# Moving the weight units and the four large operand buffers of a transformer-style trunk into one pool at the head of SBUF

## The chip, the core and the metric

The kernel runs on one core of a Trainium2 chip. The number that counts is the device time of one execution in microseconds (us). The kernel before takes 2718.81 us, the median of three runs that lie between 2717.66 and 2721.08 us. A core has a tensor engine (PE, with weight loads shown apart as PEld), a vector engine (DVE), a scalar engine (ACT), a small general engine (POOL) and a queue engine (SP) that issues the transfers between the main memory and the on-chip memory SBUF. SBUF has 128 partitions; a tile lies at the same byte address in each of them, and addresses below are bytes within a partition.

## The reference

One layer over 2048 tokens of width 1024, all in float32. Three mixers run side by side on the same normalised input, their outputs are joined by one projection, and a squared-ReLU MLP and a gated embedding follow:

```python
xn = rmsnorm(h, norm_mix_g[i])
proj = xn @ w_in[i]                                     # 1024 -> 3200 columns, split among the mixers
att = chunked_attention(qa, ka, va, qn_g[i], kn_g[i], rel_bias[i])   # 6 heads, own chunk + 8 before
conv = conformer_conv(uc, ...)                          # GLU, 31 taps, layernorm, swish, pointwise
ret = retention(qr, kr, vr, gr, ret_gn_g[i])            # 6 heads, chunkwise recurrent
h = h + jnp.concatenate([att, conv, ret], axis=-1) @ w_o[i]
hn = rmsnorm(h, norm_ffn_g[i])
h = h + jnp.square(jax.nn.relu(hn @ w1[i])) @ w2[i]     # 1024 -> 4096 -> 1024
gate = jax.nn.sigmoid(rmsnorm(h, norm_ple_g[i]) @ w_pg[i])
h = h + gate * (p[i] @ w_ple[i])
```

## The kernel before

**Blocks and segments.** The tokens are worked in four blocks of 512 (`T`). Each block is a list of segments that follow each other on the tensor engine: `conv_proj`, the two halves of `gate` of the block before, three pairs of `att_proj` and `ret_proj`, `wo_a`, `wo_b`, then the MLP as eight groups, `ffn1(g+1)` ahead of `ffn2(g)`. The small matmuls and transposes of attention, convolution and retention (`att_mix`, `conv_mix`, `ret_mix`) are put between the matmuls of these segments at places that a planner of due times chooses; the tensor engine's order is fixed by the program.

**Three matmuls for one.** A product in float32 precision is made of three float32r matmuls. Every operand is kept as a rounded high part and a remainder: `xh`, `xl` for the activations, `w[:, 0]` and `w[:, 1]` for the weights. `mm3s` issues high times high, high times low, low times high. A matmul has a stationary operand, 128 columns that are loaded by a weight load, and a moving operand, here mostly 512 columns of 4 bytes, 2048 bytes of each partition. In the names of the profile the moving operand stands first: `acc<-hid,w` has `hid` moving and `w` stationary. In the projections of attention and retention the parts change places (`acc<-w,xh`: a weight slice moves, 384 or 512 columns of it).

**Weight units.** `wunit` (line 133 on) hands out units of 8 KB a partition, two parts by two halves by 512 columns, from six buffers (`wtile`, line 122). In the first block a unit is loaded raw, split on ACT and DVE (lines 126, 127) and kept in main memory; later it is loaded in one transfer of 1 MB (`w<-k_w...`). A unit feeds eight weight blocks, 24 matmuls. A stationary block starts at the unit's address plus a multiple of 512 bytes.

**The four large buffers.** `big(name, slot)` (line 79) gives buffers of 16 KB a partition, eight rows of 2048 bytes. Slots 0 and 1 hold `xh` and `xl`: of the layer's input, of the MLP's input (`wo_b`), and in the last block of the gate's input. Slots 2 and 3 hold the mixers' output `mh` and `ml`, then in turn the hidden activations `hid` of the MLP (even groups in slot 2, odd ones in slot 3, high parts in rows 0 to 3 and low parts in rows 4 to 7), and in blocks 0 to 2 the gate's input (`late`, also named `xh`, `xl`).

**Where they lie.** Tiles of a pool lie one behind the other in the order in which their tags are first asked for, and pools in the order in which they are made. In the built program of before:

| tile | first byte | modulo 2048 |
|---|---|---|
| six weight units `w` | 23,584 to 64,544, 8192 apart | 1056 |
| slot 0 and slot 1 | 72,736 and 89,120 | 1056 |
| slot 2 and slot 3 | 195,712 and 212,096 | 1152 |
| embedding operands `ph`, `pl` | 172,640 to 178,784, 2048 apart | 608 |

Of the kernel before, what the change touches and what calls it, by code (L numbers as in the profile page):

```python
# [12 lines left out]
F32R = mybir.dt.float32r  # L13
# [4 lines left out]
P = 128  # L18
D = 1024
S = 2048  # L20
T = 512
# [11 lines left out]
HALF = 512  # L33
# [7 lines left out]
def trunk(ctx, tc, a, out):  # L41
# [4 lines left out]
    class PE:  # L46
# [10 lines left out]
        def transpose(o, x, i):  # L57
            clk[0] += 240 / 2200.0
            tc.keep_in_program_order(nc.tensor.transpose(o, x, i))  # L59

    cpool = ctx.enter_context(tc.tile_pool(name="const", bufs=1))
    sp = ctx.enter_context(tc.tile_pool(name="sp", bufs=1))
    dram = ctx.enter_context(tc.tile_pool(name="dram", bufs=1, space=bass.MemoryType.DRAM))
# [9 lines left out]
    def stile(tag, bufs, shape, name=None, dt=F32):  # L73
        return sp.tile(list(shape), dt, tag=tag, name=name or tag, bufs=bufs)
# [2 lines left out]
        return stile("raw", 2, [P, UNIT], name)  # L77

    def big(name, slot):
        return stile(f"big{slot}", 1, [P, 8, T], name, F32R)  # L80

    def anat(name):
        return stile("anat", 5, [P, 256], name)
# [36 lines left out]


    def wtile():
        return stile("w", 6, [P, 2, 2, HALF], "w", F32R)

    def wsplit(w, x, n, eng):
        A.activation(w[:, 0, :n], x, AF.Copy)  # L126
# [6 lines left out]
    def wunit(name, i, n=HALF):  # L133
        key = name + "_".join(map(str, i))
        seen[key] = seen.get(key, 0) + 1
        with tc.high_priority(offset=AHEAD):
            u = wtile()
            if key in kept:
                nc.sync.dma_start(f(u)[:, :, :, :n], kept[key])
            else:  # L140
                raw = rawt("raw")
                nc.sync.dma_start(raw[:, : 2 * n], a[name][i])
                for c in range(2):
                    wsplit(u[:, c], raw[:, c * n : c * n + n], n, V)
        if key not in kept and seen[key] == (2 if name == "w2" or key in ("wc0", "wc1") else 1):
            wstage(key, u, n)
        return [u[:, 0], u[:, 1]]
# [114 lines left out]

    def xnorm(blk):
        xh, xl = big("xh", 0), big("xl", 1)
        cur["x"] = xh, xl
        tk = slice(blk * T, blk * T + T)
# [189 lines left out]
    def mix():  # L456
        if "m" not in cur:
            cur["m"] = big("mh", 2), big("ml", 3)
        return cur["m"]
# [228 lines left out]
    def wo_b():  # L688
        mh, ml = mix()
        h = cur["h"]  # L690
        x = cur["x2"] = big("xh", 0), big("xl", 1)
        sq = cur["sq"] = rnat("sq")
        cur["r2"] = None
        w = stream("w_ob")
        for j in range(KT):
            b = wide()
            for k in range(2):
                yield from mm3s(b, w(2 * j + k), (mh[:, 6 + k], ml[:, 6 + k]), k == 0, k == 1)
                if k == 1:
                    with tc.high_priority(offset=60):  # L700
                        V.tensor_tensor(h[j], h[j], b, ALU.add)
                    rms_split(j, 1, x, sq)
                yield cost(T) / 3
        del cur["m"]
# [214 lines left out]
    first = xnorm(0)  # L919
    raw = rawt("raw")  # L920
    u = wtile()
    with tc.high_priority(offset=3 * AHEAD):
        nc.sync.dma_start(ng, a["norm_g"])
# [132 lines left out]
```

## Time and profile before

| | |
|---|---|
| median of 3 runs | 2718.81 us (2717.66 to 2721.08) |
| the profiled execution's own time | 2718.58 us |
| its span, first to last instruction | 2716.6 us |
| PE busy | 2680.4 us (99%), 13354 matmuls |
| DVE, ACT busy | 1327.8 us (49%), 764.2 us (28%) |
| transfers | 533.36 MB, mean 196 GB/s |
| mean granted clock of the tensor engine | 0.996 |

The span leaves out 2.0 us that the execution's own time has around it. A matmul of the profile has a start and a modelled end; neighbours overlap in the pipeline, so that a matmul is shown with some 390 ns although the next one starts some 230 ns later. How fast the tensor engine goes is therefore read from starts: the distance from the start of one group of matmuls to the start of the next, divided by their number. The chain of work in order of time gives its pieces just so, from start to start.

### The profile page before, as it was taken

To read this page: it belongs to the slowest core of one execution; us is meant where nothing else is said; L and a number is where in the kernel's file an instruction comes from. 1 tells how busy PE (TensorE), PEld (TensorE's weight loads), DVE (VectorE), ACT (ScalarE), POOL (GpSimd) and SP (SyncE) were. 2 spreads that over 40 slices of the span, in tenths; PEclk is the share of its full clock that TensorE was granted. 3 is DMA by queue.
4 is the path that set the end of the run, shared out by engine and by line. 5 is a ranking of instruction groups with operands and counts; after the bars stand their busy time and mean duration, and the time that the engine had idled before them with its cause. 6 is when DMAs were issued, how large, how long until landed. Compare 5 with 4: busy or idle time off the path is not lost.

```text
span 2716.6 us, 33597 instructions
## 1 busy us (share of the span) xinstructions
PE 2680.4 (99%) x13354; PEld 2216.5 (82%) x13354; DVE 1327.8 (49%) x2649; ACT 764.2 (28%) x1576; POOL 97.0 (4%) x98
## 2 busy tenths in 40 slices
PE   8989999999999999999999999999999999999999
PEld 7777788888888888888888888888888888888887
DVE  7966544458655443334755552222384545222233
ACT  4444423343244222123214331101222432110111
POOL 1010000000010000000001000000000100000000
PEclk9999999999999999999999999999999999999999
DMA  8667656467633567677543455555654354555553
GB/s 285 211 213 244 219 177 208 166 198 267 217 121 140 206 216 261 216 255 261 217 168 121 159 203 192 193 186 191 240 194 170 112 199 142 189 191 187 192 201 125
DMA packets 123708, 533.36 MB, mean 196 GB/s; under 512 B 12832, under 2 KB 39712, under 8 KB 77728
## 3 DMA queue, kind: packets, MB, share of 16 engines
q1 hardware_dynamic: 123552, 531.21, 55.7%
q8 instruction: 106, 1.74, 0.3%
q14 instruction: 50, 0.41, 0.0%
HBM read 410.58 MB, written 120.59 MB: 196 GB/s over the span
## 4 chain that ended last, share of the span: by engine, by line
PE 89%; DVE 6%; DMA 2%; POOL 1%; ACT 1%; issue 1%; SPq 0%; POOLq 0%; DVEq 0%; ACTq 0%
PE acc L54 52%; PE w L54 27%; PE ple L54 2%; PE po L54 2%; PE sc L54 2%; PE sc L59 1%; POOL ass L199 1%; PE rout L54 1%; DVE y L359 1%; PE cvp L54 1%; DMA w<-k_wr 1%; DVE w L127 1%; PE rsc L54 1%; POOL g L199 0%; PE cpw L54 0%
## 5 line engine op out<-in xcount | busy, mean ns | idle before, releaser
L54 PE MATMUL acc<-xh,w 128*128 128x512 f32 (+1 forms) x1744 | 546.7, 389 | 0.0
L54 PE MATMUL acc<-w,xh 128*128 128x512 f32 (+1 forms) x1536 | 457.5, 373 | 1.1 <-DMA w<-k_wr 1.1
L54 PEld LDWEIGHTS acc<-xh,w 128*128 128x128 f32 x1744 | 326.3, 188 | 70.5 <-ACT xh L233 0.2
L54 PE MATMUL acc<-hid,w 128*128 128x512 f32 x1536 | 373.7, 396 | 0.0
L54 PE MATMUL w<-hid,w 128*128 128x512 f32 x1536 | 368.8, 395 | 0.0
L54 PEld LDWEIGHTS w<-hid,w 128*128 128x128 f32 x1536 | 288.5, 188 | 69.9
L54 PEld LDWEIGHTS acc<-hid,w 128*128 128x128 f32 x1536 | 288.7, 188 | 69.7
L54 PE MATMUL acc<-xl,w 128*128 128x512 f32 (+1 forms) x872 | 337.4, 391 | 1.9 <-DVE xl L234 1.9
L54 PE MATMUL w<-xh,w 128*128 128x512 f32 x1024 | 323.3, 391 | 0.0
L54 PEld LDWEIGHTS acc<-w,xh 128*128 128x128 f32 x1536 | 280.8, 189 | 38.9 <-issue 6.3
L126 ACT ACTIVATE w<-raw 128x512 fp32r<-128x512 f32 (+1 forms) x288 | 163.4, 615 | 460.6 <-PE acc L54 190.3
L54 PE MATMUL acc<-w,xl 128*128 128x384 f32 (+1 forms) x768 | 284.2, 370 | 0.0
L721 ACT ACTIVATE hid<-r 128x512 fp32r<-128x512 f32 x128 | 80.0, 625 | 569.3 <-DVE r L720 569.3
L54 PEld LDWEIGHTS w<-xh,w 128*128 128x128 f32 x1024 | 192.8, 189 | 39.7
L54 PE MATMUL w<-xl,w 128*128 128x512 f32 x512 | 200.1, 391 | 0.0
L54 PEld LDWEIGHTS acc<-xl,w 128*128 128x128 f32 x872 | 163.9, 188 | 38.3 <-DVE xl L234 4.2
L127 DVE TENSOR_TENSOR w<-raw,w 128x512 fp32r<-128x512 f32 (+1 forms) x288 | 182.7, 676 | 23.8 <-ACT w L126 23.1
L747 DVE TENSOR_TENSOR h<-h,w 128x512 f32<-128x512 f32 x128 | 88.0, 687 | 205.7 <-PE w L54 205.3
L359 DVE SCALAR_TENSOR_TENSOR y<-gl,cw,y 128x512 f32<-128x512 f32 x240 | 172.5, 745 | 1.9
L747 DVE TENSOR_TENSOR h<-h,acc 128x512 f32<-128x512 f32 x128 | 87.9, 687 | 169.9 <-PE acc L54 169.5
L54 PEld LDWEIGHTS acc<-w,xl 128*128 128x128 f32 x768 | 145.5, 189 | 15.7 <-issue 0.5
L720 DVE SCALAR_TENSOR_TENSOR r<-acc,r 128x512 f32<-128x512 f32 x64 | 44.3, 691 | 210.6 <-PE acc L54 197.7
(177 smaller groups left out, 2811.9 us busy)
## 6 DMA issues: line engine op xcount, KB each, us to landing
w<-k_w SPq DMA_DIRECT2D x160, 1024.0 KB, 4.8
k_w<-w SPq DMA_DIRECT2D x64, 1024.0 KB, 7.1
raw<-in_w_dram SPq DMA_DIRECT2D x96, 512.0 KB, 4.4
w<-k_wr SPq DMA_DIRECT2D x36, 1024.0 KB, 7.1
w<-k_w_g SPq DMA_DIRECT2D x30, 1024.0 KB, 4.8
w<-k_wa SPq DMA_DIRECT2D x36, 768.0 KB, 5.6
w<-k_w_oa SPq DMA_DIRECT2D x18, 1024.0 KB, 7.0
k_wr<-w SPq DMA_DIRECT2D x12, 1024.0 KB, 7.3
```

The source lines that it names most:

```text
L54: tc.keep_in_program_order(nc.tensor.matmul(o, x, y, start=start, stop=stop))
L59: tc.keep_in_program_order(nc.tensor.transpose(o, x, i))
L126: A.activation(w[:, 0, :n], x, AF.Copy)
L127: eng.tensor_tensor(w[:, 1, :n], x, f(w[:, 0, :n]), ALU.subtract)
L199: G.tensor_tensor(o, var, nhalf[:, :n], ALU.pow)
L359: V.scalar_tensor_tensor(y, gl[:, j : j + T], cw[:, c, j : j + 1], y, ALU.mult, ALU.add)
L720: V.scalar_tensor_tensor(r, b, 0.0, cur["r2"], ALU.max, ALU.mult)
L721: A.activation(hid[:, j], r, AF.Square)
L747: V.tensor_tensor(h[j], h[j], b, ALU.add)
```

## The change

A new pool `gp` is made ahead of all others, and the tags of the weight units and of the four large buffers move into it. Sizes and numbers of buffers stay as they were.

```diff
+    gp = ctx.enter_context(tc.tile_pool(name="gp", bufs=1))
     cpool = ctx.enter_context(tc.tile_pool(name="const", bufs=1))
     sp = ctx.enter_context(tc.tile_pool(name="sp", bufs=1))
...
     def big(name, slot):
-        return stile(f"big{slot}", 1, [P, 8, T], name, F32R)
+        return gp.tile([P, 8, T], F32R, tag=f"big{slot}", name=name, bufs=1)
...
     def wtile():
-        return stile("w", 6, [P, 2, 2, HALF], "w", F32R)
+        return gp.tile([P, 2, 2, HALF], F32R, tag="w", name="w", bufs=6)
```

The instructions of every engine, their order and the semaphores that they wait for are the same in the two built programs; the SBUF addresses are all that differs. In the changed program:

| tile | first byte | modulo 2048 | was |
|---|---|---|---|
| six weight units `w` | 1,152 to 42,112, 8192 apart | 1152 | 1056 |
| slot 0 and slot 1 | 50,304 and 66,688 | 1152 | 1056 |
| slot 2 and slot 3 | 83,072 and 99,456 | 1152 | 1152 |

Everything else moves by a whole number of 2048 bytes or stays where it was (constants, the raw weights and the small tiles ahead of the old slot 0 by 114,688, what lay between the old slots 1 and 2 by 32,768), so its address modulo 2048 is unchanged.

## Rows read from the trace of the kernel before

**Rows 1.** The page, busy time, share of the span and instructions of each engine.
```profile
PE 2680.4 (99%) x13354; PEld 2216.5 (82%) x13354; DVE 1327.8 (49%) x2649; ACT 764.2 (28%) x1576; POOL 97.0 (4%) x98
```
**Rows 2.** The page, chain that ended last, by engine.
```profile
PE 89%; DVE 6%; DMA 2%; POOL 1%; ACT 1%; issue 1%; SPq 0%; POOLq 0%; DVEq 0%; ACTq 0%
```
**Rows 3.** Timeline of PE in block 1's MLP: start, us to the last end.
```profile
1001.59 5.76 PE L54 MATMUL w<-hid,w 128*128 128x512 f32 x24
1007.19 5.76 PE L54 MATMUL acc<-hid,w 128*128 128x512 f32 x24
1012.79 5.76 PE L54 MATMUL w<-hid,w 128*128 128x512 f32 x24
```
**Rows 4.** Chain in order of time, same MLP: start, us until the next piece.
```profile
1018.55 8.28 PE acc L54 x36
1026.83 10.88 PE w L54 x48
1037.71 8.25 PE acc L54 x36
...
1062.77 8.28 PE acc L54 x36
```
**Rows 5.** Chain in order of time, gate of block 0, operands in slots 2 and 3.
```profile
680.05 5.60 PE acc L54 x24
685.65 1.38 PE ple L54 x6
687.03 5.60 PE acc L54 x24
```
**Rows 6.** Chain in order of time, gate of block 3, operands in slots 0 and 1.
```profile
2670.94 5.49 PE acc L54 x24
2676.43 1.39 PE ple L54 x6
2677.82 5.49 PE acc L54 x24
```
**Rows 7.** Chain in order of time, wo_a and wo_b of block 1.
```profile
926.17 17.73 PE acc L54 x76
943.90 2.80 PE w L54 x12
```
**Rows 8.** Groups of instructions by line and shape: xcount, busy us, mean ns, idle.
```profile
L54 PE MATMUL acc<-xh,w 128*128 128x512 f32 x1712 | 540.7, 391 | 0.0
L54 PE MATMUL acc<-hid,w 128*128 128x512 f32 x1536 | 373.7, 396 | 0.0
L54 PE MATMUL w<-hid,w 128*128 128x512 f32 x1536 | 368.8, 395 | 0.0
L54 PE MATMUL acc<-xl,w 128*128 128x512 f32 x856 | 332.9, 393 | 1.9 <-DVE xl L234 1.9
L54 PE MATMUL w<-xh,w 128*128 128x512 f32 x1024 | 323.3, 391 | 0.0
L54 PE MATMUL acc<-w,xh 128*128 128x512 f32 x768 | 249.7, 402 | 1.1 <-DMA w<-k_wr 1.1
L54 PE MATMUL acc<-w,xh 128*128 128x384 f32 x768 | 207.8, 345 | 0.0
L54 PE MATMUL w<-xl,w 128*128 128x512 f32 x512 | 200.1, 391 | 0.0
L54 PE MATMUL acc<-w,xl 128*128 128x512 f32 x384 | 152.6, 398 | 0.0
L54 PE MATMUL acc<-w,xl 128*128 128x384 f32 x384 | 131.5, 343 | 0.0
```
**Rows 9.** Busy time by stretch in the MLP; last three: clock, DMA share, GB/s.
```profile
1000.00:1100.00 100.00, 100.00 (x435) 81.48 (x434) 35.67 (x53) 18.87 (x34) 0.00 (x0) 1.00 0.66 232
```
**Rows 10.** The page, DMA issues: KB each, us from issue to landing.
```profile
w<-k_w SPq DMA_DIRECT2D x160, 1024.0 KB, 4.8
```

## The prediction

> **What bounds the kernel now.** I read the shares of busy time first: PE is busy 99% of the span, DVE 49%, ACT 28% [rows 1]. The chain that ended last says the same from the other side: 89% of the span is PE's own work [rows 2]. So the kernel is as fast as matmuls follow one another, and an edit that moves no instruction can change the time only through that distance. I therefore read starts, not durations, in the timeline and in the chain in order of time.
>
> The reader is to see that the distance is not the same everywhere although the matmuls are: 128 rows, 128 columns, 512 moving columns each time. In the MLP, runs of 24 matmuls over `hid` start at 1001.59, 1007.19 and 1012.79: 5.60 us for 24, which is 233.3 ns [rows 3]. The run of 48 (a run over `hid` has at most 24, so this is `ffn1`, over `xh` and `xl`) takes 10.88 us: 226.7 ns [rows 4]. The two kinds alternate every 22 us under the same load from the other engines, with the same weight buffers and result banks. What differs is where the moving operand lies: `xh`, `xl` at 1056 modulo 2048 like the weights, `hid` at 1152, which is 96 bytes off.
>
> The gate gives the same comparison with one and the same code. In block 0 its operand is in slots 2 and 3, and 24 matmuls take 5.60 us [rows 5]; in block 3 it is in slots 0 and 1, and they take 5.49 us [rows 6]. `wo_a` and `wo_b`, whose operand is in slots 2 and 3, need 17.73 us for 76 and 2.80 us for 12, 233.3 ns both times [rows 7]. And the six matmuls over `ph`, `pl`, at 608, take 1.38 us, 230 ns [rows 5]. So every operand that lies otherwise than the weights takes 230 ns or more here, and the ones that lie as the weights do take about 227.
>
> **The change part by part.** It removes, adds and reorders nothing: the sum has terms for distances between matmuls alone. What I suppose, and the rows don't prove, is that the distance depends on how the moving operand and the weight block that is loaded meanwhile lie to each other; then 226.7 ns holds for all of them after the change.
>
> - MLP. One period of the chain, from 1018.55 to 1062.77, is 44.22 us and holds 96 matmuls over `xh`, `xl` and 96 over `hid` [rows 4]. At 226.7 ns all 192 take 43.52 us: 0.70 us less. There are 32 periods (4 blocks by 8 groups; 3072 matmuls over `hid` [rows 8], 96 each): 22.3 us.
> - Gate of blocks 0 to 2. 3 blocks by 8 columns, each with a run of 24: I take the measured difference of the two gates, 5.60 - 5.49 = 0.11 us [rows 5, 6], not the full 24 x 6.6 ns = 0.16, because the run in block 3 also stands behind six `ple` matmuls and yet needs 5.49 where 24 at 226.7 ns would need 5.44. 24 x 0.11 = 2.6 us; bounds 0 and 3.8.
> - `wo_a`, `wo_b`. 76 matmuls in one unbroken piece and 48 of `wo_b` (8 columns, 2 steps, 3 matmuls) a block go at 233.3 ns [rows 7]. 4 x 124 x 6.6 ns = 3.3 us; the other 68 of `wo_a` stand between transposes and small matmuls, and I count nothing for them. Bounds 0 and 5.1 (all 768 matmuls); I take 3.3.
> - `ple`. 198 matmuls whose operand stays at 608 while the weights go from 1056 to 1152. No row shows that distance. By the nearest rows it lies between 226.7 and 233.3 ns against 230 now: 198 x 3.3 ns, 0.7 us up or down. I take 0.
> - The segments that go at 227 ns now (`conv_proj`, the projections, `ffn1`, the gate of block 3). Operands and weights move together, so their distance to each other stays; I take 0. That is the dear assumption, and the second rival prices it.
> - Cover. If the MLP goes 1.6% faster, its weights must come 1.6% sooner: a unit of 1 MB feeds 24 matmuls, 5.44 us then, and lands 4.8 us after its issue [rows 10] with six buffers; DMA is at 0.66 and DVE at 36% there [rows 9]. Neither becomes late. The waits of the mixers' stages hang on DVE and ACT chains between segments that I leave as they are: 0.
>
> The sum is 22.3 + 2.6 + 3.3 = 28.2 us off the execution's own 2718.58 us (span 2716.6 us): 2690.4. That execution is 0.2 us below the median of the runs, so for the median I say 2691 us, 1.0% faster.
>
> [...]
>
> **The rivals.**
>
> *The address is not what counts; nothing changes.* Then `hid` and the gate of block 0 would need their 233 ns for a reason of their stages, and the time stays at 2718.6 us. For it: I know the addresses from the built program and only infer that they act. Against it: pieces of both paces alternate in the MLP, and the gate has both paces with the same code [rows 5, 6]. [...]
>
> *The address itself counts, not the distance; slower.* Here a start at 1056 would be good in itself and one at 1152 bad, whatever the weights do: the rows near 233 ns are all at 1152 or 608, those near 227 all at 1056, and no row has weights and operand together at 1152. Then `ffn1`, `conv_proj`, the projections and the gate of block 3 take 233.3 ns too. Moving `xh`, `xl` (1712 + 856 + 1024 + 512 less the 576 of the early gates, from [rows 8]): 3528 x 6.6 ns = 23.3 us. Moving weights (768 + 384 of 512 columns, as many of 384 [rows 8]): 2304, of which I take half, since these stand among transposes: 1152 x 6.6 = 7.6 us. Sum 31 us, 2750 us. It decides from the pace that all matmuls then share: 3072 + 496 + 400 matmuls win up to it and 3528 + 1152 lose from it, which is even at 229.7 ns. Against it: 1152 is the rounder address (9 x 128), and 1056 would have to be special among 608, 1056 and 1152 by accident just where the weights lie as well.
>
> *It comes half way.* The pace after the change is better but not 226.7: say 229 to 230 ns for `hid`, as the 228.8 ns of the gate in block 3 and the 230 of `ple` show that paces between exist. The 28 us become 10 to 16: 2703 to 2709 us.
>
> *Distance from the low end of SBUF.* All operands with 230 ns and more lie above 172,000, all with 227 below 106,000. If that is the cause, the change brings the four buffers below 116,000 and the result is that of the forecast. It shares its number, and only an experiment would tell them apart.
>
> **How the numbers follow.** Forecast, by relative or by low address, 0.68 at 2691 (its own range 2683 to 2700: the bounds of gate, `wo` and `ple` together, some 9 us). Half way 0.08. Nothing 0.09. Slower by the address itself 0.15. A measurement of this kernel tells 0.2% (5.4 us) from no change, so forecast and half way are faster (0.76), nothing is the same (0.09), the last is slower (0.15). The range reaches from 2683 to 2721 and so takes in half way and nothing; outside are the slower case and a few hundredths at the low end.
>
> **What would show it.** In the profile after: runs of 24 over `hid` at 5.44 us from start to start instead of 5.60; MLP periods of 43.5 instead of 44.2; runs of 48 over `xh`, `xl` still 10.88; the gate of block 0 at about 5.49. Runs of 48 at 11.2 us would mean that the address itself counts, and runs of 24 still at 5.60 beside 10.88 that nothing has been removed. The prediction is wrong if PE's distances are as I say and the time has not fallen: then a wait has appeared in the chain that I hold to be covered.

## The result and the profile after

The changed kernel takes 2690.06 us, the median of four runs between 2688.96 and 2690.76 us, against 2718.23 us, the median of four runs of the kernel before: a ratio of 0.9895, 95% interval 0.9877 to 0.9912. The prediction said 2691 us. The profiled execution took 2690.76 us, with a span of 2688.7 us, 27.9 us less than before.

The page, busy time, share of the span and instructions of each engine, answers to [rows 1]:

```profile
PE 2651.4 (99%) x13354; PEld 2214.9 (82%) x13354; DVE 1326.3 (49%) x2649; ACT 764.1 (28%) x1576; POOL 97.0 (4%) x98
```

The same 13354 matmuls; PE's busy time has fallen by 29.0 us and nobody else's by more than 1.6. The time came from PE alone. Where on PE is read from starts again. The timeline of PE in the MLP of block 1 (start, us to the last end), beside [rows 3]:

```profile
994.16 5.60 PE L54 MATMUL w<-hid,w 128*128 128x512 f32 x24
999.60 5.60 PE L54 MATMUL acc<-hid,w 128*128 128x512 f32 x24
1005.04 5.60 PE L54 MATMUL w<-hid,w 128*128 128x512 f32 x24
```

The starts of the runs over `hid` are 5.44 us apart, where they were 5.60: 226.7 ns a matmul instead of 233.3. (The second column, 5.60, is the length to the end of the last matmul and no pace.) The chain in order of time (start, us until the next piece) shows the whole period, beside [rows 4]:

```profile
1010.64 8.16 PE acc L54 x36
1018.80 10.88 PE w L54 x48
1029.68 8.16 PE acc L54 x36
...
1054.16 8.16 PE acc L54 x36
```

The run of 48 over `xh`, `xl` is the 10.88 us that it was; the period has gone from 44.22 to 43.52 us. In 32 periods that is 22.4 us. The gates of block 0 and of block 3, beside [rows 5] and [rows 6]:

```profile
672.20 1.40 PE ple L54 x6
673.60 5.46 PE acc L54 x24
679.07 1.40 PE ple L54 x6
680.47 5.46 PE acc L54 x24
```

```profile
2648.59 1.40 PE ple L54 x6
2649.99 5.47 PE acc L54 x24
2655.46 1.40 PE ple L54 x6
2656.86 5.46 PE acc L54 x24
```

Block 0 has gone from 5.60 to 5.46 us, the two gates are now the same, and `ple` has become a little slower, 1.40 us for six. `wo_a` and `wo_b`, beside [rows 7]:

```profile
919.54 17.29 PE acc L54 x76
936.83 2.72 PE w L54 x12
```

17.73 has become 17.29 and 2.80 has become 2.72. No new wait has come into the chain: the longest that PE has for another engine is the one at the start for the first split weights (waited for, us in total, times, longest), here before and after:

```profile
PE cvp L54 <- ACT w L126: 7.0, 1, 7.0
```

```profile
PE cvp L54 <- ACT w L127: 7.7, 1, 7.7
```

All of PE's waits for other engines and transfers add up to 33.0 us, where they were 31.8. That is about the 1.1 us by which PE's busy time fell further than the span.

### The profile page after: what moved, and what is told of

It is laid out like the page before. It is cut to its first block, busy times and chain, and to the rows that moved or that the text cites. A ratio compares the mean times of both kernels' runs of the same rounds, so it can differ in the third digit from the quotient of the medians.

```text
span 2688.7 us, 33597 instructions
## 1 busy us (share of the span) xinstructions
PE 2651.4 (99%) x13354; PEld 2214.9 (82%) x13354; DVE 1326.3 (49%) x2649; ACT 764.1 (28%) x1576; POOL 97.0 (4%) x98
## 4 chain that ended last, share of the span: by engine, by line
PE 90%; DVE 5%; POOL 1%; DMA 1%; ACT 1%; issue 1%; SPq 0%; POOLq 0%; DVEq 0%; ACTq 0%
PE acc L54 53%; PE w L54 27%; PE ple L54 2%; PE po L54 2%; PE sc L54 2%; PE sc L59 2%; POOL ass L200 1%; PE rout L54 1%; PE cvp L54 1%; DVE y L360 1%; DVE w L128 1%; PE rsc L54 1%; DMA w<-k_wr 1%; POOL g L200 0%; PE cpw L54 0%
## 5 line engine op out<-in xcount | busy, mean ns | idle before, releaser
L54 PE MATMUL acc<-hid,w 128*128 128x512 f32 x1536 | 363.1, 389 | 0.0
L54 PE MATMUL w<-hid,w 128*128 128x512 f32 x1536 | 358.6, 389 | 0.0
```

What stands on the lines that cost most here:

```text
L54: tc.keep_in_program_order(nc.tensor.matmul(o, x, y, start=start, stop=stop))
```

## Experiments

Three things were open: whether the distance from the weights counts or something else that moved along with it; whether it is a distance from the weights or among the moving operands; and which distances are good.

**Matched, but far.** This kernel takes the change back and makes the match in another way: three small tiles are asked for ahead of the weights, so that weights and slots 0 and 1 start 96 bytes later, at 1152 modulo 2048, where slots 2 and 3 lie anyway, still at the high end (195,712 and 212,096).

```diff
+    stile("nm", 3, [P, 1])
     first = xnorm(0)
```

> The kernel before, with three 4-byte tiles taken ahead of the weights, so that weights and slots 0, 1 start at 1152 modulo 2048; slots 2 and 3 stay at 195,712 and 212,096, which is 1152 too. Distance theory: hid runs of 24 take 5.44 us and the time is that of the changed kernel, about 2690 us. Low-end theory (buffers above 172,000 are slow): hid stays at 5.60 us and the time at 2718 us. If a start at 1152 were bad by itself, runs of 48 over xh, xl would take 11.2 us and the time would be 2750 us; the changed kernel has shown that it is not.

Measured: 2689.4 us, ratio to before 0.9898 (0.9884 to 0.9913). The chain in the MLP of block 1:

```profile
1004.01 5.44 PE w L54 x24
1009.46 8.16 PE acc L54 x36
1017.62 10.88 PE w L54 x48
```

The whole gain is there without one buffer having come lower. The low-end rival is out. So is the rival of the start itself: in both kernels weights and large buffers lie at 1152, and the MLP goes at 226.7 ns, the pace that `xh`, `xl` had at 1056.

**Near, but 96 bytes off.** The opposite: the changed kernel, with 96 bytes between slot 1 and slot 2.

```diff
+    gp.tile([P, 24], F32, tag="pad", name="pad", bufs=1)
     seen["wc0"] = 1
```

> The changed kernel with 96 bytes between slot 1 and slot 2, so that slots 2 and 3 lie low (83,168 and 99,552) but 96 bytes off the weights, as before. Distance theory: hid runs of 24 take 5.60 us, 76 matmuls of wo_a 17.7 us, the time goes back to 2718 us. Low-end theory: 5.44 us and 2690 us.

Measured: 2717.95 us, ratio to before 1.0003 (0.9993 to 1.0012). Chain in the MLP, and `wo_a`:

```profile
1013.43 5.60 PE w L54 x24
1019.03 8.28 PE acc L54 x36
1027.31 10.88 PE w L54 x48
```

```profile
926.66 17.73 PE acc L54 x76
```

The 96 bytes alone give back the whole gain, place for place. (A pad in the first pool moves all that lies behind it by its length, the embedding operands too; this holds for all the kernels with a pad.)

**The weights off, the buffers agreeing.** The pad of 96 bytes stands between the weights and slot 0.

```diff
     u = wtile()
+    gp.tile([P, 24], F32, tag="pad", name="pad", bufs=1)
```

> The changed kernel with 96 bytes between the weights and slot 0: the four buffers agree among themselves and none agrees with the weights. Distance from weights counts: hid 5.60 us for 24 and xh, xl 11.2 us for 48, gates 5.60, time 2690 + 28 + 31 = 2749 us. What counts is that the moving operands agree with each other: 5.44 and 10.88 us, 2690 us.

Measured: 2743.13 us, ratio to before 1.0095 (1.008 to 1.011). Chain in the MLP:

```profile
1017.71 5.60 PE w L54 x24
1023.31 8.40 PE acc L54 x36
1031.71 11.20 PE w L54 x48
```

Now `xh`, `xl` pay as well, 11.20 us for 48, although all moving operands agree with each other. It is the distance between moving and stationary operand that counts.

The time is 53 us above the changed kernel, not 59: the term for the projections, in which the weights move, was too large. A stretch of 45 of their matmuls in block 2 shows where, in this kernel and then in the changed one (the starts of the first matmul of 384 columns, of the first of 512, and of what follows them; the lines between are left out):

```profile
1543.81 0.61 PE L54 MATMUL acc<-w,xh 128*128 128x384 f32 x2
1547.04 0.62 PE L54 MATMUL acc<-w,xh 128*128 128x512 f32 x2
1553.35 0.60 PE L59 MATMUL roT<-ident,ro 128*128 128x128 f32 x4
```

```profile
1519.71 0.62 PE L54 MATMUL acc<-w,xh 128*128 128x384 f32 x2
1522.94 0.63 PE L54 MATMUL acc<-w,xh 128*128 128x512 f32 x2
1529.11 0.60 PE L59 MATMUL roT<-ident,ro 128*128 128x128 f32 x4
```

The 18 matmuls of 384 columns take 3.23 us in both: there the 96 bytes cost nothing. The 27 of 512 columns take 6.31 us instead of 6.17. Added up over all their starts, the projections take some 2 us more, where 7.6 had been counted; in the profile their busy time is 744.4 us against 741.3, and the time leaves 1.6 us for them (53.1 less 28.2 for the lost gain and 23.3 for `xh`, `xl`).

**Other distances.** The same pad between slots 1 and 2, of 32, 64, 128, 256 and 512 bytes, one run each.

```diff
+    gp.tile([P, 128], F32, tag="pad", name="pad", bufs=1)    # 512 bytes; 64, 32, 16 and 8 for the others
     seen["wc0"] = 1
```

> The changed kernel with 512 bytes between slot 1 and slot 2. The weight blocks lie 512 bytes apart, and all four of them went at 226.7 ns with a moving operand at the unit's own start. If only the distance modulo 512 counts: hid 5.44 us for 24 matmuls, 2690 us. If the distance modulo 2 KB counts, as the change's words say: about 5.60 us and 2718 us.

> The changed kernel with 256 bytes between slot 1 and slot 2. If the pace repeats every 256 bytes or less: 5.44 us for 24 over hid, 2690 us. If only a multiple of 512 is good: about 5.60 us and 2718 us.

> The changed kernel with 128 bytes between slot 1 and slot 2. So far 0, 256 and 512 bytes gave 5.44 us for 24 over hid, 32 and 96 gave 5.60, 64 gave 5.49. If the pace repeats every 128 bytes: 5.44 us and 2690 us. If it repeats every 256 bytes, 128 may be anything from 5.44 to 5.60 us, 2690 to 2718 us.

> The changed kernel with 64 bytes between slot 1 and slot 2, the distance that ph had from the weights in the kernel before, where six matmuls took 1.38 us (230 ns). If the pace is a function of the distance: 24 over hid take 5.52 us, the time is 2704 us. If every distance but zero costs the same: 5.60 us and 2718 us.

> The changed kernel with 32 bytes between slot 1 and slot 2, the smallest step that the pools give. If the pace grows with the distance: below 5.52 us for 24 over hid, under 2704 us. If every distance but zero costs the same: 5.60 us and 2718 us.

One run of 24 over `hid` in the MLP of block 1, in this order: 512, 256, 128, 64 and 32 bytes.

```profile
1004.88 5.44 PE w L54 x24
```

```profile
1004.28 5.44 PE w L54 x24
```

```profile
1011.20 5.60 PE w L54 x24
```

```profile
1008.70 5.49 PE w L54 x24
```

```profile
1011.88 5.60 PE w L54 x24
```

| distance, bytes | 24 over `hid`, us | time, us |
|---|---|---|
| 0 (changed kernel) | 5.44 | 2690.06 |
| 32 | 5.60 | 2716.71 |
| 64 | 5.49 | 2701.46 |
| 96 | 5.60 | 2717.95 |
| 128 | 5.60 | 2717.94 |
| 256 | 5.44 | 2689.29 |
| 512 | 5.44 | 2690.0 |

Agreement modulo 2048, as the tables of addresses compare it, is more than is needed: 256 and 512 bytes are as good as none. The pace does not grow with the distance, and 128 bytes, a rounder step than 64, are worse; a period of 128 is out. Distances between 128 and 256 were not tried for `hid`. My own expectations for 32 and 64 were written for two laws, growth and all-or-nothing, and neither holds: 32 bytes cost all of it and 64 less than half (11.4 of some 28 us).

**Only the low part off.** One run. Slot 1, which holds `xl`, is moved 32 bytes off the weights; slot 0 is at 0 and slots 2 and 3 are at 512 from them. In `xnorm`:

```diff
-        xh, xl = big("xh", 0), big("xl", 1)
+        xh = big("xh", 0)
+        if blk == 0:
+            gp.tile([P, 8], F32, tag="pad", name="pad", bufs=1)
+        xl = big("xl", 1)
+        if blk == 0:
+            gp.tile([P, 120], F32, tag="pad2", name="pad2", bufs=1)
```

> The changed kernel with 32 bytes between slot 0 and slot 1 and 480 between slot 1 and slot 2: of all large buffers only slot 1, which holds the low parts xl, is off the weights; slots 2 and 3 are 512 bytes off. Each matmul pays for its own distance: one in three of the runs over xh, xl is slower, 48 take 10.88 + 16 x 0.0066 = 10.99 us, about 1176 matmuls, 2698 us. One operand off sets the pace of its neighbours: 48 take 11.2 us, 2713 us.

Measured: 2713.47 us. The chain in the MLP, then the 45 matmuls of the projections in block 2, here and in the changed kernel:

```profile
1013.92 5.44 PE w L54 x24
1019.36 8.28 PE acc L54 x36
1027.64 11.12 PE w L54 x48
```

```profile
1532.30 9.69 PE acc L54 x45
```

```profile
1519.78 9.49 PE acc L54 x45
```

48 over `xh`, `xl` take 11.12 us, 0.24 more than 10.88 and twice what one matmul in three could cost by itself (0.11). So a matmul that is off disturbs its neighbours, too. That the total falls on the second theory's 2713 us is in part luck. Its 11.20 us for 48 did not come: at 0.24 us for 48 the 3528 matmuls over `xh`, `xl` lose 17.6 us, not 23.3. Most of the rest comes from the projections, where `xl` is stationary and for which it counted nothing: the 45 shown lose 0.20 us, and the busy time of all of them in the profile is 748.5 us against 741.3.

**One more mismatch.** `ph` and `pl` of `ple` lie in `rnat` tiles. Here these are moved to the first pool as well.

```diff
-        return stile("rnat", 4, [P, 512], name)
+        return gp.tile([P, 512], F32, tag="rnat", name=name, bufs=4)
```

> The changed kernel with the four tiles that hold ph and pl in the first pool too, at 1152 like the weights. Distance theory: the runs of 6 over ph, pl go from 1.40 us to 1.36, and the gate runs of 24 behind them from 5.465 to 5.44 us; 32 of each, 33 x 0.04 + 32 x 0.025 = 2.1 us less, 2688 us. If ple needs 233 ns for another reason (its result bank, its place between two runs): no change, 2690 us.

Measured: 2688.89 us, ratio to before 0.9892 (0.9875 to 0.9908). The chain in the gate of block 0:

```profile
668.00 5.44 PE acc L54 x24
673.44 1.36 PE ple L54 x6
674.80 5.44 PE acc L54 x24
680.24 1.36 PE ple L54 x6
```

The rows are as expected to the hundredth: 226.7 ns in the MLP, in `wo_b` and in the gates, and 17.29 us for the 76 of `wo_a`, as in the changed kernel. Whether the time follows needs the changed kernel beside it, on one chip:

> The changed kernel, timed on the same chip as the next one: 2690 us by both theories.

> The kernel with ph and pl at the weights' address too, beside the changed kernel on one chip: 2.1 us less than it by the distance theory (its profile showed runs of 1.36 and 5.44 us instead of 1.40 and 5.465), no difference if something later takes it back.

Measured: 2690.12 us (2689.09 to 2691.01) for the changed kernel, ratio to before 0.9897 (0.9882 to 0.9913), and 2686.24 us (2684.82 to 2689.04) with `ph` and `pl` matched, 0.9887 (0.9869 to 0.9904). The two sets of four don't overlap; over the eight runs of each the medians are 2690.06 and 2687.84 us, 2.2 us apart, where 2.1 were worked out. The two intervals to before overlap widely, though, and 0.08% is less than the 0.15 to 0.18% by which each of them reaches to either side. Part of it may be the clock: three of the eight runs with `ph` and `pl` matched, 2684.82 to 2685.36 us, had a mean granted clock of 0.998 or 0.999, where six of the changed kernel's eight had 0.996 or 0.997. This version is the best one found; the pace in its rows is shown, the gain in time is not.

The kernel with 32 bytes has a last piece of it. Its `rnat` tiles lie 32 bytes on as well, at 640 modulo 2048, which is 512 bytes from the weights, so `ple` is matched there and the runs around it are not:

```profile
677.50 1.39 PE ple L54 x6
678.89 5.60 PE acc L54 x24
```

Six matched matmuls between mismatched ones take 1.39 us, not 1.36: the loss carries over to matched neighbours. How far it reaches can be read in the gate of block 0 of the changed kernel, where 24 matched matmuls stand behind six mismatched ones (the starts of the first, the sixth and the last; the lines between are left out):

```profile
673.44 0.39 PE L54 MATMUL acc<-xh,w 128*128 128x512 f32 x1
674.60 0.62 PE L54 MATMUL acc<-xh,w 128*128 128x512 f32 x2
678.68 0.39 PE L54 MATMUL acc<-xh,w 128*128 128x512 f32 x1
```

The first five take 1.16 us, 232 ns each, and the next eighteen 4.08 us, 226.7 ns each: the loss dies away behind its cause.

## Why the prediction was right

Point by point, by its own steps:

- **Bound.** PE's distances were the whole of the gain: PE's busy time fell by 29.0 us and the span by 27.9.
- **MLP.** 22.3 us were said; the period fell from 44.22 to 43.52 us, which is 22.4.
- **Gate of blocks 0 to 2.** 2.6 us were said, at 0.11 us a run. It was 5.60 less 5.46 or 5.47, some 0.135, 3.2 us. I had taken the loss in block 3 for one that `ple` leaves behind and that stays as it was; it shrank with the new distance of `ph`, `pl`, and the gate of block 3 won 0.02 to 0.03 us in most of its runs too.
- **`wo_a`, `wo_b`.** 3.3 us were said. 76 matmuls won 0.44 us and each 12 of `wo_b` 0.08, with four such pieces a block: 4 x (0.44 + 0.32) = 3.0. The other 68 of `wo_a`, for which nothing was counted, won too: added up over the starts of all 768 matmuls it is 3.9 us.
- **`ple`.** Nothing was said, with 0.7 us either way. 198 matmuls went from 230 to 233 ns, 1.38 or 1.39 to 1.40 us for six: 33 x 0.015 = 0.5 us lost, inside its bounds.
- **What goes at 227 ns now stays so.** The dear assumption held: 10.88 us for 48.
- **Cover.** Held: no wait in the chain that was not there. The waits that were there grew by 1.2 us in all, for which nothing was said; 0.7 of it is the one at the start. Whether the change has a part in it, no run shows.

The sum of the pieces, 22.4 + 3.2 + 3.9 - 0.5, is 29.0 us, what PE's busy time fell by; less 1.2 us of waiting it is 27.8, as the profiled executions differ. The medians differ by 28.2. That the distance to the weights counts was right, but that the total is right to 1 us is in part luck: the gate and `wo_a`, `wo_b` were put 1.2 us too low together, and `ple` and the waits, put at nothing, took 1.7 us back.

The supposition under it, relative position and not place, is shown by three kernels for matmuls of 512 columns with weights stationary: matched and far (5.44 us for 24 over `hid`), near and off (5.60), weights off alone (5.60, and 11.20 for 48 over `xh`, `xl` instead of 10.88). Whether it is the weight block in use or, as I supposed, the one loaded meanwhile, no run tells, since all weight blocks lie multiples of 512 bytes apart. What the rows show is the pace alone: 96 bytes between the two operands make 24 matmuls 5.60 us long instead of 5.44. Which part of the chip makes it so, no run here shows.

Of the rivals, "nothing changes" fell with the result. "The address itself" fell with it too; its price was 2750 us, and the kernel that has all buffers off took 2743.1: no run shows the mechanism of that rival, and its term for moving weights, 7.6 us, was sized too large: in the kernel with the weights off the projections lost some 2 us, and their matmuls of 384 columns nothing in the stretch shown. The term had taken half of them because they stand among transposes; the stretch shows the number of columns instead. "Distance from the low end" had the forecast's number and was told apart only by the kernel that is matched and far. "Half way" did not happen at 0 bytes; 64 bytes come near it, 229 ns and 2701.46 us where 2703 to 2709 were said.

## What to carry to other kernels

Where matmuls bound the kernel, compare the distance from start to start between groups of the same shape; a few ns between groups that differ only in the tile they read (here 233.3 against 226.7) point to where the tiles lie. Put the stationary operands and the moving operands at one address modulo 256 bytes (here 24 matmuls took 5.44 us at distances of 0, 256 and 512 bytes, 5.49 at 64 and 5.60 at 32, 96 and 128), and every small operand that stands between them too (here six over `ph`, `pl` went from 1.40 us to 1.36 and the 24 behind them from 5.46 to 5.44), and check the addresses of the built program, because 96 bytes between two large tiles cost 1% here (2717.95 us against 2690.06). Test it by a pad in either direction: it costs a line, and it tells the relative place from the absolute one. All of this was seen with matmuls of 128 rows and 512 columns of 4 bytes, each with a weight load of its own (13354 of each in the profile); the shorter ones of 384 columns lost nothing at 96 bytes in the stretch shown, 3.23 us for 18 in both kernels.

## What the runs showed of the hardware that was not expected

The pace has no simple law in the distance: 226.7 ns at 0, 256 and 512 bytes, 229 at 64, 233.3 at 32, 96 and 128. It is not a price of each matmul by itself, because the loss reaches matched neighbours: with `xl` alone off, 48 matmuls lose 0.24 us where their 16 off ones could lose 0.11; six matched ones between mismatched runs take 1.39 us instead of 1.36; and behind six mismatched ones five matched ones go at 232 ns before the pace is 226.7 again. Why it reaches so far, no run shows.
